# Normed rows transposed by halves of the tokens, and a first chunk that takes the first 256 tokens first

## The chip, the cores and the metric

One core of a Trainium2 chip runs the whole program in one launch. The metric is the device time of one execution in microseconds (us); the kernel before took 3114.05 us, the median of three runs (3106.38 to 3122.09).

## The reference

Two blocks of two layers on 512 tokens of 1024 features, in fp32. What matters here is what stands between the layers: the sum of a layer's input and output is normed row by row, and the next layer begins with a matrix product of these rows.

```python
def layer_norm(x, g, b):
    mu = mean(x, -1); var = mean(square(x - mu), -1)
    return (x - mu) * rsqrt(var + LN_EPS) * g + b

h = layer_norm(x, ln_in_g, ln_in_b)                      # passage 1
for l in range(2):                                       # first block
    hcat = h @ w_in[l] + b_in[l]                         # 7168 columns, attention and gating on them
    ...
    h = layer_norm(ALPHA * h + merged @ w_out[l] + b_out[l], ln_g[l], ln_b[l])   # passages 2 and 3
for l in range(2):                                       # second block
    p = h @ w_in_2[l]                                    # four recurrent mixers on its columns
    ...
    h = layer_norm(ALPHA * h + mix, ln1_g[l], ln1_b[l])  # passages 4 and 6
    f = swiglu(h) if l == 0 else moe(h)
    h = layer_norm(ALPHA * h + f, ln2_g[l], ln2_b[l])    # passage 5, and the output
```

So there are six passages from normed rows into a product with weights. The sixth goes into the router of the mixture of experts.

## The kernel before

Rows of the 512 tokens lie in four tiles of 128 tokens, `H[t][0]` and `H[t][1]`, each 128x512 (512 features). Products want the features on the partitions, so every normed tile is transposed on TensorE, eight blocks of 128x128 a tile, into PSUM banks (`norm_transpose`, L495). A bank holds 128x512, one block `k` of 128 features for all 512 tokens; seven banks are open at once, and the eighth block waits for one to come free. An fp32 product is made of three fp32r products: `split` (L412 to L415) casts a transposed block to a high part `hh` on ScalarE and subtracts it for a low part `hl` on VectorE; `weights` (L384) loads a chunk of 1024x256 as two transfers of 512 KB, casts each to `wh` on ScalarE (L395) and subtracts for `wl` on VectorE (L399); `mm3` (L406 to L408) multiplies `wh` by `hh`, `wh` by `hl` and `wl` by `hh`. (In the trace's names the operands stand as they come: L407 reads `hl`, L408 reads `wl`.) `proj_f` takes one half of a chunk, 128 output features, through all eight blocks: 24 matmuls of 512 columns into one of two PSUM banks of the tag `mm`.

The norm of a tile (`norm_rows`, `norm_apply`) runs over all engines: VectorE's statistics (L543, L1457 and their like) and aggregation (L454), the power on GpSimd (L439), then for the first half of the features two operations on VectorE (L467, L468) and for the second half one on ScalarE (L355), a product on GpSimd (L470) and a sum on VectorE (L485). `norm_end` then scales the rows (L515, ScalarE), adds a bias row at some passages (L518, GpSimd) and writes them to memory (L520, SyncE's queue), for the next residual.

Each engine runs its instructions in one order, written by a scheduler at build time that models when each could start. `BEHIND`, `FREE` and `HELD` (L33 to L35) steer it: the first `wl` of the first chunk is free, the next four are held behind the split number `BEHIND`. What follows the first chunk: at passages 1 and 2 `naqkv` (L592, VectorE), at 3 and 5 `shift` (L1513 on ScalarE, L1515 to L1517 on VectorE), at 4 a Silu on ScalarE (L355). These read the two `mm` banks and free them.

Of the kernel before, what the change touches and what calls it, by code (L numbers as in the profile page):

```python
# [19 lines left out]
P = 128  # L20
D = 1024
S = 512
KT = D // P
# [4 lines left out]
CW = 256  # L28
# [6 lines left out]
BEHIND = 3  # L35
# [5 lines left out]
PF, PS = (0, 1), (0,)  # L41
# [218 lines left out]
def _consts3():  # L260
# [16 lines left out]
T_R, T_K, T_V, T_WA, T_G, T_HF, T_HQ, T_LQ, T_LK, T_LR, T_HG, T_RQ, T_RK, T_RG = (  # L277
    0, 2, 4, 6, 7, 8, 10, 12, 13, 14, 16, 18, 20, 22)
# [36 lines left out]
class K:  # L315
# [104 lines left out]
    def proj_f(self, w, c0, hT, kt=KT):  # L420
# [4 lines left out]
            self.mm3(o, w[k][0][:, c0:c0 + P], w[k][1][:, c0:c0 + P], hh[:, k, :], hl[:, k, :], k == 0, k == kt - 1)  # L425
        return o

    def proj_t(self, w, width, t, hT, kt=KT, tag="mm"):

        o = self.bank(tag)  # L430
        hh, hl = hT
        for k in range(kt):
            self.mm3(o[:, :width], hh[:, k, t * P:(t + 1) * P], hl[:, k, t * P:(t + 1) * P],
                     *w[k], k == 0, k == kt - 1)
        return o[:, :width]
# [3 lines left out]
        self.nc.gpsimd.tensor_tensor(out, out, self.mhalf, op=ALU.pow)  # L439
        return i.ins  # L440

    def norm_begin(self, ng, nb, bo=None, keep=None, spill=False, tags="tsatsamt", pool=()):

        banks = [{"t": "tp", "s": "sc", "a": "av", "m": "mm"}[c] for c in tags]
        self.ln = SimpleNamespace(g=self.row(ng), b=self.row(nb), bo=None if bo is None else self.row(bo),
                                  keep=keep, spill=spill, tags=banks, tp={}, pool=pool, late=None,
                                  mv=self.xp.tile([P, 4, 2], F32, name="mv", tag="mv", bufs=2),
                                  rs=self.xp.tile([P, 4], F32, name="rs", tag="rs", bufs=2),
                                  sh=self.xp.tile([P, 4], F32, name="sh", tag="sh", bufs=2))
# [37 lines left out]
            for j in range(2):  # L487
                nc.sync.dma_start(ln.keep[j][t * P:(t + 1) * P, :], H[t][j])

    def norm_transpose(self, t, ks=range(7)):  # L490
        ln = self.ln
        for k in ks:
            if k not in ln.tp:
                ln.tp[k] = self.bank(ln.tags[k])
            self.nc.tensor.transpose(ln.tp[k][:, t * P:(t + 1) * P], self.H[t][k // 4][:, (k % 4) * P:(k % 4 + 1) * P],  # L495
                                     self.ident)

    def norm_end(self):

        nc, ln, H = self.nc, self.ln, self.H  # L500
        hh = self.xp.tile([P, KT, S], F32R, name="hh", tag="hh")
        hl = self.xp.tile([P, KT, S], F32R, name="hl", tag="hl")
        for t in range(4):
            self.norm_transpose(t)
        for k in range(KT):
            if k >= 7:
                for t in range(4):
                    self.norm_transpose(t, [k])
            i = self.split(hh[:, k, :], hl[:, k, :], ln.tp[k])
            if k == BEHIND:  # L510
                self.behind = (i.ins, FREE, HELD)
        for t in range(4):
            for j in range(2):
                h = H[t][j]
                nc.scalar.mul(h, h, ALPHA)  # L515
                if ln.bo is not None:
                    with self.tc.issue_after(ln.last_mul):
                        nc.gpsimd.tensor_add(h, h, ln.bo[j])  # L518
                if ln.spill:
                    nc.sync.dma_start(self.hd[j][t * P:(t + 1) * P, :], h)  # L520
        return hh, hl
# [49 lines left out]
    def hybrid(self, l, hT):  # L571
        nc, aps = self.nc, self.aps
# [12 lines left out]
        nq, nk, nv = [], [], []  # L585
        for c in range(0, 12, 2):
            w = chunk(c)
            for j in range(2):
                o = self.proj_f(w, j * P, hT)
                t = self.c("naqkv")  # L590
                (nq if c < 4 else nk if c < 8 else nv).append(t)
                nc.vector.tensor_scalar(t.rearrange("p (c r) -> p r c", r=8), o.rearrange("p (r c) -> p r c", c=64),  # L592
                                        bcol(c + j), -0.125 if c < 4 else 1.0, op0=ALU.add, op1=ALU.mult)
# [237 lines left out]
        nb = R_L + 5 * l  # L831
        self.norm_begin(nb, nb + 1, nb + 5 + 2 if l + 1 < DEPTH else None, spill=True)
        st = self.stats()
        for js in ((0,), (1,), (2, 3)):
            w = [self.weights(aps[f"wo1_{l}"][j], KT, CW) for j in js]
# [37 lines left out]
    def second_block(self, hT):  # L873
        nc, aps = self.nc, self.aps
        cst = self.cp.tile([P, 1154], F32, name="cst2")
        nc.sync.dma_start(cst, aps["cst2"][:, :1154])
        self.perm, self.blk1, self.cen = cst[:, 0:128], cst[:, 128:256], cst[:, 256:384]
        self.masks = cst[:, 384:512], cst[:, 512:640]
        self.reset = cst[:, 640:1152]
        self.sign = cst[:, 1152:1153]  # L880
        msk = self.cp.tile([P, 8 * P], mybir.dt.uint8, name="msk")
        for c0 in range(0, 8 * P, S):
            nc.gpsimd.tensor_copy(msk[:, c0:c0 + S], self.load(aps["msk2"][:, c0:c0 + S]))
        self.lvt = lambda n: msk[:, (1 + n) * P:(2 + n) * P]

        m64 = self.cp.tile([P, 12, 64], mybir.dt.uint8, name="m64")
        self.strict64 = self.cp.tile([P, 64], F32, name="strict64")
        nc.sync.dma_start(self.strict64, aps["cst3"][:, :64])
        nc.gpsimd.tensor_copy(m64[:, 6:12].rearrange("p n c -> p (n c)"), self.load(aps["cst3"][:, 64:448])[:, :384])
        self.ident64 = self.cp.tile([P, 64], F32, name="ident64")  # L890
        for h in (slice(0, 64), slice(64, P)):
            nc.gpsimd.tensor_copy(m64[h, :6], msk[h, P:7 * P].rearrange("p (n c) -> p n c", c=P)[:, :, h])
            nc.gpsimd.tensor_copy(self.ident64[h], self.ident[h, h])
        self.lvt64 = lambda n: m64[:, n]
        self.lv64 = lambda n: m64[:, 6 + n]
        self.fcol = {}
        for name, val in (("m_rms", RMS_EPS), ("m_ln", LN_EPS), ("m_lnx", 64e-5), ("one", 1.0),
                          ("b15", 15 * float(np.log(2.0)))):
            t = self.cp.tile([P, 1], F32, name=name)
            nc.vector.memset(t, val)  # L900
            self.fcol[name] = t
        self.ones = self.cp.tile([P, P], F32, name="ones")
        nc.vector.memset(self.ones, 1.0)
        h4 = self.cp.tile([P, 4], F32, name="h4")
        nc.vector.memset(h4, 0.0)
        for h in range(4):
            nc.vector.memset(h4[32 * h:32 * h + 32, h:h + 1], 1.0)
        self.heads = {2: self.blk1.rearrange("p (h c) -> p c h", c=64)[:, 0], 4: h4}
        self.rotary_tables()
        self.lower_bound()  # L910
        for l in range(DEPTH):
            v0 = V2_L + l * V2_LN
            self.v2 = lambda n, i=0, w=1: self.vec[:, v0 + V2[n] + i:v0 + V2[n] + i + w]
            self.hv2 = lambda n, i=0, w=1: self.hvec[:, v0 + V2[n] + i:v0 + V2[n] + i + w]
            nb = R2_L + 4 * l
            if l == 1:
                self.moe_begin()
            hT = self.mixers(l, hT)
            if l == 0:
                for i in range(2):  # L920
                    hT_ = self.swiglu(hT, aps[f"fgu_{i}"], aps[f"fd_{i}"], (nb + 2, nb + 3) if i else None)
                hT = hT_
            else:
                self.moe(hT, (nb + 2, nb + 3))
# [391 lines left out]
                put(main * P, P, j, y)  # L1316
                put(rest_col * P + own, R, j, t[:R])

    def swiglu(self, hT, wgu, wd, norm):

        nc = self.nc
        ah, al = [], []
        for m in range(11):
            w = self.weights(wgu[m], KT, CW)
            g = self.proj_f(w, 0, hT)
            s = self.tmp()
            self.act(s, g, AF.Silu)
            u = self.proj_f(w, P, hT)
            nc.vector.tensor_mul(s, s, u)
            ah.append(self.c("ah", F32R))  # L1330
            al.append(self.c("al", F32R))
            self.split(ah[m], al[m], s)
        if norm:
            self.norm_begin(*norm, spill=True, tags="smsmaatt", pool=PS)
            st = self.xp.tile([P, 4, 2, 6], F32, name="st2", tag="st2", bufs=2)
        acc = {}
        order = [[(j, k0, kn)] for j in range(2) for k0, kn in ((0, 3), (3, 4))] + [[(0, 7, 4), (1, 7, 4)]]
        for part in order:
            w = [self.weights(wd[j][:, k0 * 512:(k0 + kn) * 512], kn, 512) for j, k0, kn in part]
            for t in range(4):  # L1340
                for (j, k0, kn), wj in zip(part, w):
                    if k0 == 0:
                        acc[j, t] = self.bank((("mm", "mm", "sc", "sc"), ("av", "av", "tp", "tp"))[j][t])
                    for k in range(kn):
                        ts = slice(t * P, t * P + P)
# [13 lines left out]
    def mixers(self, l, hT):  # L1359

        nc, aps = self.nc, self.aps
# [4 lines left out]
        hold = {}  # L1366
        self.y = {}

        def feat(t):
            if t % 2 == 0:  # L1370
                hold["w"] = self.weights(wf[t // 2], KT, CW)
            return self.proj_f(hold["w"], (t % 2) * P, hT)

        def tok(i, out):
            w = self.weights(aps[f"w2t_{l}"][i], KT, CW)
# [9 lines left out]
        k = [self.shift(feat(T_K + i), mu(2 + i)) for i in range(2)]  # L1385
# [9 lines left out]
        z = self.rwkv_common(v, wa, g1, g2)  # L1395
# [627 lines left out]
```

## Time and profile before

| | |
|---|---|
| median of 3 runs | 3114.05 us |
| the profiled execution's own time | 3123.69 us |
| its span | 3121.9 us |
| TensorE clock granted, mean | 0.968 |
| TensorE busy | 2969.5 us (95%) |
| VectorE busy | 1881.3 us (60%) |
| ScalarE busy | 1314.5 us (42%) |
| GpSimd busy | 357.0 us (11%) |

The six passages lie in the trace at 14 to 42, 605 to 629, 1198 to 1220, 1630 to 1654, 2006 to 2030 and 2437 to 2454 us: from about the last product of the old layer to the end of the first chunk of the new one. Times within the trace are from the start of the span. A row's duration reaches some 0.08 us into the next row of a busy engine, so that the pitch of a run of instructions is read from their starts.

### The profile page before, as it was taken

What the parts mean: (1) busy time and instruction counts of PE and PEld (TensorE: products, weight loads), DVE (VectorE), ACT (ScalarE), POOL (GpSimd) and SP (SyncE); (2) the same over time, 40 slices, a digit from 0 to 9 for tenths busy, and PEclk for the clock granted to TensorE, in tenths of its full rate; (3) what the DMA queues carried; (4) which work ended last, traced back from release to release, by engine and by line L of the source; (5) the groups of instructions that cost most, each with busy time, mean ns of one, the idle gap of its engine ahead of it and who ended that gap; (6) DMA issues with size and microseconds to landing.
All of it is one profiled execution on the core that took longest, in us unless ns stands there. A gap on an engine that the chain in (4) does not pass through costs nothing. (4 is left out here: it accounts for less than half of the span.)

```text
span 3121.9 us, 46921 instructions
## 1 busy us (share of the span) xinstructions
PE 2969.5 (95%) x18729; PEld 2426.4 (78%) x18729; DVE 1881.3 (60%) x3318; ACT 1314.5 (42%) x2257; POOL 357.0 (11%) x377
## 2 busy tenths in 40 slices
PE   7999999999999999998999999999999799999987
PEld 5688788877878888786668888778775699999973
DVE  6676554657745566636574333555467777777765
ACT  3534332335433333524433222343354466666642
POOL 3220000211100001004210000100232200000021
PEclk9999999999999999999899999999999899999997
DMA  5322224242221333210303233321121378777772
GB/s 187 103 81 81 71 65 148 79 148 78 75 80 49 122 122 115 75 41 16 102 28 101 88 102 95 130 90 43 35 68 62 130 250 265 255 250 258 250 260 87
DMA packets 116535, 365.69 MB, mean 117 GB/s; under 512 B 13585, under 2 KB 16785, under 8 KB 116305
## 3 DMA queue, kind: packets, MB, share of 16 engines
q1 hardware_dynamic: 113424, 353.13, 35.0%
q0 software_dynamic: 2880, 9.44, 0.9%
q8 instruction: 150, 2.46, 0.3%
q14 instruction: 81, 0.66, 0.1%
HBM read 344.83 MB, written 17.69 MB: 116 GB/s over the span
## 5 line engine op out<-in xcount | busy, mean ns | idle before, releaser
L399 DVE TENSOR_TENSOR wl<-wr,wh 128x1024 fp32r<-128x1024 f32 (+1 forms) x574 | 696.9, 1223 | 519.6 <-ACT wh L395 514.0
L395 ACT CAST wh<-wr 128x1024 fp32r<-128x1024 f32 (+1 forms) x574 | 594.2, 1045 | 754.0 <-PE mm L407 340.3
L406 PE MATMUL mm<-hh,wh 128*128 128x512 f32 (+1 forms) x1616 | 652.2, 404 | 0.1
L407 PE MATMUL mm<-hl,wh 128*128 128x512 f32 (+1 forms) x1616 | 645.2, 399 | 0.0
L408 PE MATMUL mm<-hh,wl 128*128 128x512 f32 (+1 forms) x1616 | 642.0, 398 | 0.1
L406 PEld LDWEIGHTS mm<-hh,wh 128*128 128x128 f32 (+1 forms) x1616 | 306.3, 190 | 75.0 <-issue 7.1
L408 PEld LDWEIGHTS mm<-hh,wl 128*128 128x128 f32 (+1 forms) x1616 | 305.7, 189 | 73.3 <-issue 4.3
L407 PEld LDWEIGHTS mm<-hl,wh 128*128 128x128 f32 (+1 forms) x1616 | 306.1, 189 | 69.9 <-issue 5.6
L1266 PE MATMUL mm<-xgT,wh 128*128 128x320 f32 x704 | 219.1, 311 | 2.1 <-issue 2.1
L1266 PE MATMUL sc<-xgT,wh 128*128 128x320 f32 x704 | 218.7, 311 | 1.1 <-issue 1.1
L1267 PE MATMUL mm<-xgT,wl 128*128 128x256 f32 x704 | 197.6, 281 | 4.1 <-issue 4.1
L1267 PE MATMUL sc<-xgT,wl 128*128 128x256 f32 x704 | 197.6, 281 | 2.7 <-issue 2.7
L1266 PEld LDWEIGHTS mm<-xgT,wh 128*128 128x128 f32 x704 | 133.1, 189 | 4.3 <-issue 3.6
L1266 PEld LDWEIGHTS sc<-xgT,wh 128*128 128x128 f32 x704 | 133.1, 189 | 4.2 <-issue 4.2
L1267 PEld LDWEIGHTS mm<-xgT,wl 128*128 128x128 f32 x704 | 133.3, 189 | 2.3 <-issue 2.0
L1267 PEld LDWEIGHTS sc<-xgT,wl 128*128 128x128 f32 x704 | 133.0, 189 | 2.3 <-issue 2.3
L406 PE MATMUL mm<-wh,hh 128*128 128x256 f32 x448 | 130.8, 292 | 0.6 <-DVE sgv L754 0.6
L439 POOL TENSOR_TENSOR rs<-rs,mhalf 128x1 f32<-128x1 f32 x36 | 29.7, 824 | 889.3 <-DVE rs L438 858.8
L407 PE MATMUL mm<-wl,hh 128*128 128x256 f32 x448 | 129.2, 288 | 0.0
L408 PE MATMUL mm<-wh,hl 128*128 128x256 f32 x448 | 128.4, 287 | 0.0
L728 DVE TENSOR_REDUCE mn<-sc 128x1 f32<-128x512 f32 x64 | 44.1, 689 | 86.0 <-PE sc L725 85.7
L355 ACT ACTIVATE tmp<-mm,hvec 128x512 f32<-128x512 f32 x72 | 49.4, 686 | 96.1 <-PE mm L408 96.1
(554 smaller groups left out, 5674.8 us busy)
## 6 DMA issues: line engine op xcount, KB each, us to landing
wr<-mgu SPq DMA_DIRECT2D x176, 512.0 KB
wr<-w SPq DMA_DIRECT2D x172, 512.0 KB
wr<-md SPq DMA_DIRECT2D x88, 512.0 KB
wr<-fgu SPq DMA_DIRECT2D x44, 512.0 KB
wr<-wo SPq DMA_DIRECT2D x32, 512.0 KB
wr<-wbr SPq DMA_DIRECT2D x24, 512.0 KB
row<-rows SPq DMA_DIRECT2D x40, 256.0 KB
wr<-fd SPq DMA_DIRECT2D x20, 512.0 KB
```

Source lines behind the costliest of these rows:

```text
L355: i = self.nc.scalar.activation(out, src, f, **kw)
L395: nc.scalar.copy(hi[:, :n], raw[:, :n])
L399: nc.vector.tensor_sub(lo[:, :n], raw[:, :n], hi[:, :n].bitcast(F32))
L406: mm(out, lh, rh, start=first, stop=False)
L407: mm(out, lh, rl, start=False, stop=False)
L408: mm(out, ll, rh, start=False, stop=last)
L439: self.nc.gpsimd.tensor_tensor(out, out, self.mhalf, op=ALU.pow)
L728: nc.vector.tensor_reduce(mx[u][:, a:a + 1], sc, axis=AX.X, op=ALU.min)
L1266: mm(o[i][:, :2 * CAP], wh, x[:, k, :2 * CAP], start=k == 0, stop=False)
L1267: mm(o[i][:, :256], wl, x[:, k, :256], start=False, stop=k == KT - 1)
```

## The change

A bank now holds two blocks of 128 features for 256 tokens: bank (half, kp) takes blocks 2kp and 2kp+1 of the tokens of tiles 0 and 1, or 2 and 3. `norm_end` transposes tiles 0 and 1, splits their four banks, then transposes tiles 2 and 3 and splits theirs: eight splits of 128x2x256 in place of eight of 128x512. `self.behind` is set to the last split of the first half. A new function, `proj_first`, takes both halves of a first chunk together, the first 256 tokens through all blocks, then the last 256: 96 matmuls of 256 columns in place of 48 of 512, in two `mm` banks that are both open to its end. It is called at passages 1 to 5; the router of passage 6 is as it was, but takes its rows through the new `norm_end`.

```diff
+    def proj_first(self, w, hT):
+        o = [self.bank("mm") for _ in range(2)]
+        hh, hl = hT
+        for n in range(2):
+            ts = slice(n * CW, (n + 1) * CW)
+            for k in range(KT):
+                for j in range(2):
+                    self.mm3(o[j][:, ts], *(x[:, j * P:(j + 1) * P] for x in w[k]), hh[:, k, ts], hl[:, k, ts],
+                             k == 0, k == KT - 1)
+        return o
...
-    def norm_begin(self, ng, nb, bo=None, keep=None, spill=False, tags="tsatsamt", pool=()):
+    def norm_begin(self, ng, nb, bo=None, keep=None, spill=False, tags="ttssaatt", pool=()):
...
-    def norm_transpose(self, t, ks=range(7)):
+    def norm_transpose(self, t):
         ln = self.ln
-        for k in ks:
-            if k not in ln.tp:
-                ln.tp[k] = self.bank(ln.tags[k])
-            self.nc.tensor.transpose(ln.tp[k][:, t * P:(t + 1) * P], self.H[t][k // 4][:, (k % 4) * P:(k % 4 + 1) * P],
+        for k in range(KT):
+            z = t // 2, k // 2
+            if z not in ln.tp:
+                ln.tp[z] = self.bank(ln.tags[4 * z[0] + z[1]])
+            c = 2 * (k % 2) + t % 2
+            self.nc.tensor.transpose(ln.tp[z][:, c * P:(c + 1) * P], self.H[t][k // 4][:, (k % 4) * P:(k % 4 + 1) * P],
                                      self.ident)
...
-        for t in range(4):
-            self.norm_transpose(t)
-        for k in range(KT):
-            if k >= 7:
-                for t in range(4):
-                    self.norm_transpose(t, [k])
-            i = self.split(hh[:, k, :], hl[:, k, :], ln.tp[k])
-            if k == BEHIND:
+        for half in range(2):
+            for t in (2 * half, 2 * half + 1):
+                self.norm_transpose(t)
+            for kp in range(4):
+                hi, lo = (x[:, 2 * kp:2 * kp + 2, half * CW:(half + 1) * CW] for x in (hh, hl))
+                i = self.split(hi, lo, ln.tp[half, kp].rearrange("p (k n) -> p k n", k=2))
+            if half == 0:
                 self.behind = (i.ins, FREE, HELD)
...
             w = chunk(c)
+            first = self.proj_first(w, hT) if c == 0 else None
             for j in range(2):
-                o = self.proj_f(w, j * P, hT)
+                o = first[j] if first else self.proj_f(w, j * P, hT)
...
-            g = self.proj_f(w, 0, hT)
+            if m == 0 and new:
+                g, u = self.proj_first(w, hT)
+            else:
+                g, u = self.proj_f(w, 0, hT), None
             s = self.tmp()
             self.act(s, g, AF.Silu)
-            u = self.proj_f(w, P, hT)
+            u = u or self.proj_f(w, P, hT)
...
-            return self.proj_f(hold["w"], (t % 2) * P, hT)
+                if t == T_R:
+                    hold["o"] = self.proj_first(hold["w"], hT)
+            return hold["o"][t - T_R] if t < T_R + 2 else self.proj_f(hold["w"], (t % 2) * P, hT)
```

What the scheduler makes of it is seen in the order of each engine. The line numbers after the change are higher: L467, L468 and L485 become L479, L480 and L497, L438 and L454 become L450 and L466, L458 becomes L470, L515 becomes L530. In the three places below `hh` and `hl` are the high and low parts of the rows, `wh` and `wl` those of the weights, `tp`, `sc`, `av` and `mm` are tags of PSUM banks, and `x4` says that four such instructions follow each other.

First, ScalarE at passage 1. Before, the cast of the first chunk's weights stands ahead of the eight casts of rows:

```order
L515 ACTIVATE H<-H 128x512
L395 CAST wh<-wr 128x1024
L515 ACTIVATE H<-H 128x512
L414 CAST hh<-tp 128x512
L414 CAST hh<-sc 128x512
L414 CAST hh<-av 128x512
```

Now, on the same engine, it stands behind all of them and behind the scalings of the rows:

```order
L530 ACTIVATE H<-H 128x512 x2
L414 CAST hh<-tp 128x2x256
L355 ACTIVATE H<-H,sh,rs 128x512
L414 CAST hh<-tp 128x2x256
L414 CAST hh<-sc 128x2x256 x2
L530 ACTIVATE H<-H 128x512
L414 CAST hh<-av 128x2x256 x2
L414 CAST hh<-tp 128x2x256 x2
L530 ACTIVATE H<-H 128x512 x5
L395 CAST wh<-wr 128x1024 x4
```

What moved is the first `wh`, from ahead of the first `hh` to behind the last scaling.

Second, VectorE at passage 1. Before, with the first `wl` ahead of the splits:

```order
L468 SCALAR_TENSOR_TENSOR H<-H,rs,row 128x512
L485 TENSOR_TENSOR H<-H,row 128x512
L399 TENSOR_TENSOR wl<-wr,wh 128x1024
L415 TENSOR_TENSOR hl<-tp,hh 128x512
L415 TENSOR_TENSOR hl<-sc,hh 128x512
L415 TENSOR_TENSOR hl<-av,hh 128x512
```

Now, VectorE from the last tile's sum (L497) to the weights of the first two chunks:

```order
L497 TENSOR_TENSOR H<-H,row 128x512
L415 TENSOR_TENSOR hl<-tp,hh 128x2x256
L415 TENSOR_TENSOR hl<-sc,hh 128x2x256 x2
L415 TENSOR_TENSOR hl<-av,hh 128x2x256 x2
L415 TENSOR_TENSOR hl<-tp,hh 128x2x256 x2
L597 TENSOR_SCALAR qg<-vec 128x1 x2
L984 TENSOR_TENSOR lbt<-vec 128x2
L1622 TENSOR_SCALAR oma<-vec 128x1 x2
L985 TENSOR_TENSOR lbt<-vec,lbt 128x2
L986 TENSOR_TENSOR lbt<-vec,lbt 128x2
L1008 TENSOR_TENSOR fold<-cst 16x8
L399 TENSOR_TENSOR wl<-wr,wh 128x1024 x4
```

Here the first `wl` moved behind the splits and behind a row of small operations on tables; one split stands ahead of L480 of the last tile, seven behind its sum. Six operations on tables and then the third chunk's `wl` follow, and only then the first `naqkv`.

Third, VectorE at passage 4, from the last tile's residual sum. Before:

```order
L1455 TENSOR_TENSOR H<-mm,H 128x512
L1457 BN_STATS st_13224<-H 128x6
L454 BN_AGGR mv<-st_13224 128x2
L438 TENSOR_SCALAR rs<-mv 128x1
L485 TENSOR_TENSOR H<-H,row 128x512
L458 SCALAR_TENSOR_TENSOR sh<-mv,rs 128x1
L467 SCALAR_TENSOR_TENSOR H<-H,mv,row 128x512
L468 SCALAR_TENSOR_TENSOR H<-H,rs,row 128x512
L485 TENSOR_TENSOR H<-H,row 128x512
L415 TENSOR_TENSOR hl<-tp,hh 128x512
```

Now, on the same engine and from the same sum:

```order
L1476 TENSOR_TENSOR H<-mm,H 128x512
L1478 BN_STATS st_13368<-H 128x6
L415 TENSOR_TENSOR hl<-tp,hh 128x2x256
L466 BN_AGGR mv<-st_13368 128x2
L415 TENSOR_TENSOR hl<-tp,hh 128x2x256
L450 TENSOR_SCALAR rs<-mv 128x1
L497 TENSOR_TENSOR H<-H,row 128x512
L470 SCALAR_TENSOR_TENSOR sh<-mv,rs 128x1
L479 SCALAR_TENSOR_TENSOR H<-H,mv,row 128x512
L415 TENSOR_TENSOR hl<-sc,hh 128x2x256
L480 SCALAR_TENSOR_TENSOR H<-H,rs,row 128x512
L497 TENSOR_TENSOR H<-H,row 128x512
```

Three splits of the first half moved between the steps of the last tile's norm; the other five come behind its last sum, and behind those the `wl` of the chunk's second half. Passages 5 and 6 have the same three splits there; passages 2 and 3 have one, between L479 and L480. On TensorE, at passages 4 and 5, 28 of the 96 matmuls of `proj_first` stand ahead of the first one that reads the second half of `wl`, and nearly as many ahead of the last tile's last four transposes; at 2 and 3 there are 11 ahead of these. At passages 3 and 5 VectorE runs L1536, L1537 and L1536 of both banks before the first L1538 that frees one.

## Rows read from the trace of the kernel before

**Rows 1.** The page, busy time by engine: us, share of the span, instructions

```profile
PE 2969.5 (95%) x18729; PEld 2426.4 (78%) x18729; DVE 1881.3 (60%) x3318; ACT 1314.5 (42%) x2257; POOL 357.0 (11%) x377
```

**Rows 2.** Waits of PE: line waited for, us in total, times, longest

```profile
PE sc L495 <- DVE H L485: 16.1, 11, 3.2
```

**Rows 3.** Timeline of PE, matmuls of 256 and 512 columns: start, us, instruction, idle before

```profile
605.48 0.28 PE L407 MATMUL mm<-wl,mh 128*128 128x256 f32 x1
605.60 0.28 PE L408 MATMUL mm<-wh,ml 128*128 128x256 f32 x1
...
625.45 0.39 PE L407 MATMUL mm<-hl,wh 128*128 128x512 f32 x1
625.68 0.39 PE L408 MATMUL mm<-hh,wl 128*128 128x512 f32 x1
```

**Rows 4.** Timeline of DVE (VectorE) at passage 1

```profile
23.52 1.75 DVE L485 TENSOR_TENSOR H<-H,row 128x512 f32<-128x512 f32 x1
25.19 2.29 DVE L399 TENSOR_TENSOR wl<-wr,wh 128x1024 fp32r<-128x1024 f32 x1
27.41 0.68 DVE L415 TENSOR_TENSOR hl<-tp,hh 128x512 fp32r<-128x512 f32 x1
...
32.19 0.85 DVE L968 TENSOR_TENSOR lbt<-vec 128x2 f32<-128x2 f32 x1
...
35.49 4.61 DVE L399 TENSOR_TENSOR wl<-wr,wh 128x1024 fp32r<-128x1024 f32 x4
```

**Rows 5.** Timeline of ACT (ScalarE) at passage 1

```profile
21.87 1.03 ACT L395 CAST wh<-wr 128x1024 fp32r<-128x1024 f32 x1
...
29.78 2.71 ACT L515 ACTIVATE H<-H 128x512 f32<-128x512 f32 x5
32.39 2.94 ACT L395 CAST wh<-wr 128x1024 fp32r<-128x1024 f32 x3
...
46.89 1.05 ACT L395 CAST wh<-wr 128x1024 fp32r<-128x1024 f32 x1 [9.28 <-DMA wr<-w]
```

**Rows 6.** Timeline of PE at passage 1

```profile
29.48 0.63 PE L408 MATMUL mm<-hh,wl 128*128 128x512 f32 x1
...
32.47 0.52 PE L406 MATMUL mm<-hh,wh 128*128 128x512 f32 x1
```

**Rows 7.** Timeline of SyncE's queue at passage 1

```profile
31.81 9.81 SPq L520 DMA_DIRECT2D hd<-H  x5
41.71 2.95 SPq L394 DMA_DIRECT2D wr<-w  x4
```

**Rows 8.** Timeline of DVE at passage 2, the second eviction of the first chunk

```profile
628.86 1.21 DVE L592 TENSOR_SCALAR naqkv<-mm,vec 128x512 f32<-128x512 f32 x1 [0.62 <-PE mm L408]
```

**Rows 9.** Timeline of DVE at passage 3, the first eviction

```profile
1217.09 0.69 DVE L1515 TENSOR_TENSOR sh<-tmp,mm 128x511 f32<-128x511 f32 x1 [2.03 <-ACT tmp L1513]
...
1217.88 0.75 DVE L1517 SCALAR_TENSOR_TENSOR sh<-sh,vec,mm 128x512 f32<-128x512 f32 x1
```

**Rows 10.** Timeline of DVE at passage 4

```profile
1637.37 0.75 DVE L468 SCALAR_TENSOR_TENSOR H<-H,rs,row 128x512 f32<-128x512 f32 x1
1639.28 0.69 DVE L485 TENSOR_TENSOR H<-H,row 128x512 f32<-128x512 f32 x1 [1.16 <-POOL H L470]
1639.89 0.68 DVE L415 TENSOR_TENSOR hl<-tp,hh 128x512 fp32r<-128x512 f32 x1
```

**Rows 11.** Timeline of POOL (GpSimd) at passage 4

```profile
1637.61 1.65 POOL L470 TENSOR_TENSOR H<-H,row 128x512 f32<-128x512 f32 x1 [1.12 <-ACT H L355]
```

**Rows 12.** Timeline of PE at passage 4

```profile
1641.87 0.78 PE L407 MATMUL mm<-hl,wh 128*128 128x512 f32 x1
...
1643.72 0.44 PE L408 MATMUL mm<-hh,wl 128*128 128x512 f32 x1
```

**Rows 13.** Timeline of DVE at passage 2, under a product on GpSimd

```profile
604.75 1.80 DVE L468 SCALAR_TENSOR_TENSOR H<-H,rs,row 128x512 f32<-128x512 f32 x1
```

**Rows 14.** Timeline of POOL at passage 2, at the same time

```profile
603.97 2.03 POOL L470 TENSOR_TENSOR H<-H,row 128x512 f32<-128x512 f32 x1 [1.12 <-ACT H L355]
```

More of the change, by code (lines that the diff above doesn't have):

```diff
@@ L920, in second_block @@
                 for i in range(2):
-                    hT_ = self.swiglu(hT, aps[f"fgu_{i}"], aps[f"fd_{i}"], (nb + 2, nb + 3) if i else None)
+                    hT_ = self.swiglu(hT, aps[f"fgu_{i}"], aps[f"fd_{i}"], (nb + 2, nb + 3) if i else None, i == 0)
                 hT = hT_
@@ L1317, in expert, with swiglu @@
                 put(rest_col * P + own, R, j, t[:R])
-    def swiglu(self, hT, wgu, wd, norm):
+    def swiglu(self, hT, wgu, wd, norm, new):
         nc = self.nc
@@ L1333, in swiglu @@
         if norm:
-            self.norm_begin(*norm, spill=True, tags="smsmaatt", pool=PS)
+            self.norm_begin(*norm, spill=True, tags="mmaasstt", pool=PS)
             st = self.xp.tile([P, 4, 2, 6], F32, name="st2", tag="st2", bufs=2)
```

## The prediction

> **What bounds the kernel now.** I read the page first: TensorE is busy 95% of the span, the other engines far less [rows 1]. A change is worth what it takes from or adds to TensorE's idle time. The waits come next: TensorE's largest wait at the norm passages is for L485 on VectorE, the sum that completes a tile, 16.1 us over 11 waits, the longest 3.2 [rows 2]. Then I read each passage engine by engine. The reader is to see there a chain: the last tile's sum on VectorE, its transposes, the splits, the weights' low part `wl`, and the first product. At passage 4 the last sum starts at 1639.28 and eight splits follow from 1639.89 [rows 10]; TensorE starts its first dense run at 1641.87, while VectorE is still splitting [rows 12]. So in the kernel before, the first product already overlaps the splits. What the change could take is the idle time before the last sum, and nothing in the product itself.
>
> **The cost of the matmuls.** 96 matmuls of 256 columns replace 48 of 512. One of 256 starts 0.12 us after the one before it (605.48 to 605.60), one of 512 0.23 us [rows 3]; over long runs 0.114 and 0.229. So the product costs the same, 11.0 us at full clock, and I put the doubled weight loads at nothing: in the stretch of 256 columns as many loads per column stand as `proj_first` has. The page "TensorE: Matmul & The Clock Gate" of the Trainium skill, in its section "Back-to-back issue gap", says that the spacing is set by load and matmul together, with a fixed part that weighs more on narrow matmuls; the trace shows no such part at 256 columns (0.12 against half of 0.23), so the sum by that rule would be the same within a microsecond a passage.
>
> Splits are as many as before and as large, eight of 128x512 elements. They write two runs of 256 rather than one of 512. I take the price of before, 0.60 us a piece on VectorE (27.41 to 32.19 is eight) [rows 4]. From below nothing makes them faster; from above, the nearest row with a split-up access is `naqkv`, 1.21 us against 0.68 [rows 8, 10]. That end is a rival below.
>
> **Passage 1, +7.0 us.** The first `wl` stood before the splits: it starts at 25.19 [rows 4], and TensorE's first L408, which reads it, at 29.48 [rows 6]. Now seven splits stand ahead of it after the last sum at 25.19: 25.2 + 7 x 0.60 = 29.4. Then the small operations, from 32.19 to 35.49, are 3.3 us [rows 4], to 32.8 with the two of `qg`; then `wl`, 1.15 (4.61 for four) [rows 4], about 34.0. Its other input is no later: the eight `hh` end by about 27.4, the five scalings take 2.6 (29.78 to 32.39), one cast of weights 1.0 [rows 5], so 31.0. L408 starts at 34.1, 4.6 late, and as the rest of the product costs the same, it ends at 46.0 in place of 41.4 (29.48, 46 matmuls at 0.229, and 1.4 us for the time to 32.47 at half clock, pitch 0.43 [rows 6]).
>
> Then both `mm` banks are full, and the first `naqkv` that frees one stands behind the third chunk's `wl`. That chunk's transfer is issued at 41.71, behind the row writes on SyncE's queue [rows 7], and its cast starts at 46.89 [rows 5], 5.2 us later. The scalings that start this chain run about 1.9 us earlier now, so I put the cast at 45.0, the cast and `wl` end at 47.2, and the eviction, 1.21 [rows 8], at 48.4: TensorE waits 2.4 us beyond 46.0. Together 7.0. Between: 6 if the transfer comes a microsecond earlier, 9 if the writes hold it as long as before. If the `wl` wait was hidden anyway, only the 2.4 is left.
>
> **Passage 2, +0.9 us (-0.5 to 2.5).** One split between L479 and L480 pushes the last tile by at most 0.6. TensorE has 11 of 96 matmuls done when the rest begins, which ends the product 0.3 earlier than before. Then it waits for one eviction, 1.21 [rows 8], which before lay beside the second half's matmuls.
>
> **Passage 3, +2.7 us (2 to 4.5).** The product ends at about the same time (+0.2). Then the first bank comes free only when ScalarE's copy, L1536 of both banks and the first L1538 are through: 0.6 for the copy, 0.60, 0.10, 0.60 and 0.70 on VectorE, pitches of the rows [rows 9]. That is 2.6, of which about 0.1 is covered. Before, the same work lay beside the second half's 5.5 us of matmuls.
>
> **Passage 4, +2.0 us (0.3 to 3).** Two splits now stand within the last tile's statistics: its sum comes 1.2 us later. A third stands ahead of L480. In the trace L468, its earlier name, starts at 1637.37 and GpSimd's product at 1637.61 [rows 10, 11], so the VectorE operation is through first; now it comes 0.6 behind the start of that product. What that costs is seen once in the trace: the same L468 takes 1.80 us rather than 0.75 [rows 10, 13] when it starts 0.78 into a product on GpSimd that ends at 606.00 [rows 14]. I take 0.5. The last sum then ends at 1639.9 + 1.7 = 1641.6, the five splits at 1644.6, `wl` of the second half at 1645.8. TensorE has 28 matmuls behind it by then, and has stood still: 68 are left, 68 x 0.116 = 7.9, to 1653.8 at full clock. Before, the product ended at 1653.7: 1641.87, 47 matmuls at 0.233, and 0.9 for the half clock until 1643.72 [rows 12]. If the clock has fallen in the wait, 1.9 is added; I take 1.5, and 0.5 for the Silu's read of the bank.
>
> The Trainium skill says the same of L480: in "SBUF — State Buffer", section "Who interferes with whom", VectorE with two operands in SBUF and GpSimd share a port that is locked for a whole instruction, the loser standing still. The trace agrees (1.80 against 0.75 above). By it the whole remaining product would be waited out, about 0.9 rather than 0.5 at passages 4 to 6, 1.2 us more in all.
>
> **Passage 5, +4.0 us (2.3 to 5).** The same delay as at 4, 1.5, and the same wait for two banks as at 3, 2.5.
>
> **Passage 6, +1.4 us (0.5 to 1.7).** The same two or three splits delay the last tile; the router has no `proj_first` that could use the early half.
>
> Where a lower end stands without a reason, it leaves out the estimated terms of that passage (the lock, the fallen clock); an upper end adds one more late operation of about 1.2 us, a `wl` [rows 4] or an eviction [rows 8].
>
> **Sum.** 7.0 + 0.9 + 2.7 + 2.0 + 4.0 + 1.4 = 18.0 us (bounds 10.6 to 25.7). On the profiled execution's 3123.69 us (span 3121.9 and 1.8 around it) that is 3141.7. This execution was 9.6 above the median, which has no part in the sum; on the median of 3114.05 it is 3132.
>
> **Rivals.** *The gain arrives (faster).* The first half's 48 matmuls, 5.5 us, run while the last tile is still being normed, at five places: 27 us less, 3087. For it: TensorE's waits for L485 (16.1 us [rows 2]) are filled, and a filled wait also keeps the clock up. Against: in VectorE's order only one split at passages 2 and 3 and three at 4 and 5 come before the last sum, so a quarter at most of the first half has its operands. I give 0.10, for 3080 to 3098.
>
> *Nothing gained, little lost (no change).* The early 28 matmuls at passages 4 and 5 keep the clock at full, so that the product ends 1 to 2 us earlier there, and the `wl` wait of passage 1 is shorter as VectorE's small operations are spread otherwise: 2.4 + 0.9 + 2.7 + 1 + 2.5 + 0.5 = 10, or as little as 5: about 3121. I give 0.25, for 3102 to 3122.
>
> *Splits are slower (more lost).* If the write or the read in two runs costs what `naqkv`'s access does, 0.53 us more a piece [rows 8, 10], five of them late at each of six passages are 16 us more: 3148. It would decide from the first split after the last sum. I give 0.10.
>
> My forecast has 0.55. Its own range is 3122 to 3146: the bounds of the sum, 3124.6 to 3139.8, and some microseconds on either side for the spread of medians.
>
> **How the numbers follow.** A difference of 0.5%, 15.6 us, is about what a measurement of this kernel can tell from no change: 3098.5 to 3129.6 is no change. Of my forecast's 0.55, 0.36 lies above 3129.6 and 0.19 below; the no-change rival adds its 0.25 to the same, the slow splits 0.10 to slower; the gain is faster: 0.10, 0.44 and 0.46. The range of 3107 to 3146 leaves out the gain and most of the slow splits.
>
> **What would show it.** In the new profile: `hl` of 128x2x256 at 0.60 apart; TensorE's first L408 at passage 1 at about 34; an idle of 2.5 us on TensorE behind the first chunk at passages 3 and 5, waiting for `sh` on VectorE; an idle of some 3 to 4 us in `proj_first` at passages 4 and 5, waiting for `wl`; the last tile's sum at passages 4 to 6 over a microsecond later after the last residual sum. I am wrong if the matmuls of the first half lie densely ahead of the last tile's transposes, or if the two banks are free when the second chunk's first matmul is due.

## The result, and the profile after

The changed kernel took 3129.80 us, the median of seven runs (3118.15 to 3136.51), against 3110.32 for the kernel before (seven runs, 3100.49 to 3122.09). The ratio is 1.0052, 95% interval 1.0032 to 1.0073: slower by 16 us (10 to 23); the two medians alone lie 19.5 apart. The forecast was 18 us slower.

The page of the profiled execution seems to say the opposite, since its span is shorter than before's 3121.9:

```profile
span 3116.3 us, 47414 instructions
PE 2955.7 (95%) x18969; PEld 2433.3 (78%) x18969; DVE 1883.1 (60%) x3318; ACT 1314.7 (42%) x2257; POOL 360.1 (12%) x377
```

That execution was the fastest of the seven. One stretch that the change doesn't touch, between passages 3 and 4, took it 9 us less than the execution of before. The windows show it, first of the kernel before, then of the changed one (us, busy time by engine, granted clock, share of the DMA engines, GB/s):

```profile
1507.00:1590.00 83.00, 76.28 (x267) 49.46 (x265) 56.81 (x139) 33.90 (x74) 19.52 (x26) 0.86 0.28 89
```

```profile
1514.00:1588.00 74.00, 67.19 (x270) 44.60 (x268) 57.08 (x139) 34.28 (x74) 20.03 (x26) 0.98 0.30 100
```

It is the same work in the same order: VectorE is busy for 57 us in both, TensorE for 76 and 67, at a granted clock of 0.86 and 0.98. In the seven profiles of the experiments below the same stretch was granted 0.98 twice, 0.93 once and 0.86 to 0.88 four times. So spans of single executions don't rank these kernels, and I compare the passages instead. The measure is the time from the start of the last tile's last statistics on VectorE to the second chunk's first matmul. At passage 3 the two ends are these rows, of the kernel before:

```profile
1200.68 0.43 DVE L529 BATCH_NORM_STATS2 st<-H 128x6 f32<-128x256 f32 x1
```

```profile
1219.94 0.39 PE L406 MATMUL mm<-hh,wh 128*128 128x512 f32 x1
```

They are 19.26 us apart. In the changed kernel the first is

```profile
1206.67 0.43 DVE L544 BATCH_NORM_STATS2 st<-H 128x6 f32<-128x256 f32 x1
```

and the second stands at 1228.64, so 21.97, and the difference is +2.71. "Product" is the same difference for the first chunk's end, "second chunk" for the second chunk's first matmul (at passage 6, with no chunk, the router's last matmul):

| passage | product | second chunk | forecast |
|---|---|---|---|
| 1 | +4.55 | +6.40 | +7.0 |
| 2 | -0.36 | +0.68 | +0.9 |
| 3 | +0.11 | +2.71 | +2.7 |
| 4 | -0.23 | +0.25 | +2.0 |
| 5 | +1.43 | +4.04 | +4.0 |
| 6 | -0.64 | -0.64 | +1.4 |
| sum | | +13.4 | +18.0 |

At passage 3 another 1.7 us come behind the second chunk's start, which makes 15.1.

Two differences lie outside these windows. Between passages 4 and 5 TensorE starts its matmuls of 512 columns 0.2333 us apart in the kernel before and 0.2289 in the changed one, at a granted clock of 1.00 in both; by passage 5 that is 2.0 us in favour of the changed kernel. Of the experiments below only halves alone has 0.2333 there too, but both spacings also turn up in other stretches from one execution to another, so that it is not shown whether the change does this. And behind passage 6 a `wl` of 1.21 us no longer stands between the router's first two operations on VectorE, which gives 0.8 us more. With both the sum is about 12.

**Passage 1.** Where the first `wl` began at 25.19 and the L408 that reads it at 29.48 [rows 4, 6], VectorE now has:

```profile
24.24 0.68 DVE L415 TENSOR_TENSOR hl<-tp,hh 128x512 fp32r<-128x512 f32 x1
...
27.24 1.27 DVE L415 TENSOR_TENSOR hl<-tp,hh 128x512 fp32r<-128x512 f32 x2
28.43 0.20 DVE L597 TENSOR_SCALAR qg<-vec 128x1 f32<-128x1 f32 x2
...
31.02 4.61 DVE L399 TENSOR_TENSOR wl<-wr,wh 128x1024 fp32r<-128x1024 f32 x4
...
44.94 1.23 DVE L399 TENSOR_TENSOR wl<-wr,wh 128x1024 fp32r<-128x1024 f32 x1 [6.42 <-ACT wh L395]
46.08 2.17 DVE L608 TENSOR_SCALAR naqkv<-mm,vec 128x512 f32<-128x512 f32 x2
```

ScalarE casts the weights for the `wl` at 44.94 when their transfer has landed:

```profile
43.86 1.05 ACT L395 CAST wh<-wr 128x1024 fp32r<-128x1024 f32 x1 [10.66 <-DMA wr<-w]
```

TensorE in that time:

```profile
31.11 0.41 PE L407 MATMUL mm<-hl,wh 128*128 128x256 f32 x1
32.28 0.80 PE L408 MATMUL mm<-hh,wl 128*128 128x256 f32 x2 [0.75 <-DVE wl L399]
...
45.38 0.28 PE L408 MATMUL mm<-hh,wl 128*128 128x256 f32 x1
47.36 0.47 PE L406 MATMUL mm<-hh,wh 128*128 128x512 f32 x1 [1.70 <-DVE naqkv L608]
```

The reader is to see both losses of the forecast: the splits and small operations ahead of `wl`, and at the end the eviction that stands behind a `wl` whose transfer was late. (The whole passage starts 0.95 us earlier in this execution: L485 at 23.52 [rows 4], L497 at 22.57.)

**Passage 3.** TensorE waits for the bank that the first L1538 frees (the profile names the L1537 before it, but TensorE goes on just behind the end of L1538 at 1228.50), then runs at the lower of its two clocks, 1.2 GHz (matmuls of 512 columns 0.43 us apart), until 1231.8:

```profile
1225.91 0.28 PE L408 MATMUL mm<-hh,wl 128*128 128x256 f32 x1
1228.64 0.77 PE L406 MATMUL mm<-hh,wh 128*128 128x512 f32 x1 [2.45 <-DVE sh L1537]
1229.21 0.63 PE L407 MATMUL mm<-hl,wh 128*128 128x512 f32 x1
...
1231.77 0.53 PE L407 MATMUL mm<-hl,wh 128*128 128x512 f32 x1
1232.13 0.39 PE L408 MATMUL mm<-hh,wl 128*128 128x512 f32 x1
```

VectorE in that time; before, L1517 of the first bank came 0.8 us behind its L1515 [rows 9], now another bank's L1536 stands between:

```profile
1226.50 0.69 DVE L1536 TENSOR_TENSOR sh<-tmp,mm 128x511 f32<-128x511 f32 x1 [0.86 <-ACT tmp L1534]
1227.10 0.15 DVE L1537 TENSOR_SCALAR sh<-tmp 128x1 f32<-128x1 f32 x1
1227.16 0.68 DVE L1536 TENSOR_TENSOR sh<-tmp,mm 128x511 f32<-128x511 f32 x1
1227.76 0.74 DVE L1538 SCALAR_TENSOR_TENSOR sh<-sh,vec,mm 128x512 f32<-128x512 f32 x1
```

**Passage 4.** VectorE, from the last tile's statistics to the second half's `wl`:

```profile
1632.24 0.69 DVE L1478 BATCH_NORM_STATS2 st<-H 128x6 f32<-128x512 f32 x1
1632.85 0.67 DVE L415 TENSOR_TENSOR hl<-tp,hh 128x512 fp32r<-128x512 f32 x1
1633.44 0.20 DVE L466 BATCH_NORM_AGGREGATE mv<-st 128x2 f32<-128x12 f32 x1
1633.56 0.64 DVE L415 TENSOR_TENSOR hl<-tp,hh 128x512 fp32r<-128x512 f32 x1
...
1636.64 1.58 DVE L480 SCALAR_TENSOR_TENSOR H<-H,rs,row 128x512 f32<-128x512 f32 x1
1638.14 0.68 DVE L497 TENSOR_TENSOR H<-H,row 128x512 f32<-128x512 f32 x1
...
1642.06 3.49 DVE L399 TENSOR_TENSOR wl<-wr,wh 128x1024 fp32r<-128x1024 f32 x3
```

TensorE had done its 28 early matmuls by then, and waited for that `wl`, 3.55 us:

```profile
1638.98 0.37 PE L407 MATMUL mm<-hl,wh 128*128 128x256 f32 x1
1639.18 0.60 PE L510 MATMUL tp<-cst,H 128*128 128x128 f32 x4
1643.33 0.50 PE L408 MATMUL mm<-hh,wl 128*128 128x256 f32 x2 [3.55 <-DVE wl L399]
1643.67 0.28 PE L406 MATMUL mm<-hh,wh 128*128 128x256 f32 x1
```

**Passage 5.** The same kind of wait, 3.23 us, but here TensorE comes out of it at 1.2 GHz (0.21 us a matmul of 256 columns):

```profile
2016.66 0.79 PE L408 MATMUL mm<-hh,wl 128*128 128x256 f32 x2 [3.23 <-DVE wl L399]
2017.25 0.41 PE L406 MATMUL mm<-hh,wh 128*128 128x256 f32 x1
2017.47 0.41 PE L407 MATMUL mm<-hl,wh 128*128 128x256 f32 x1
```

### The profile page after: what moved, and what is told of

Same layout as the page of the kernel before. It is cut to its first block, busy times and chain, and to the rows that moved or that the text cites. A ratio compares the mean times of both kernels' runs of the same rounds, so it can differ in the third digit from the quotient of the medians.

```text
span 3116.3 us, 47414 instructions
## 1 busy us (share of the span) xinstructions
PE 2955.7 (95%) x18969; PEld 2433.3 (78%) x18969; DVE 1883.1 (60%) x3318; ACT 1314.7 (42%) x2257; POOL 360.1 (12%) x377
## 5 line engine op out<-in xcount | busy, mean ns | idle before, releaser
L406 PE MATMUL mm<-hh,wh 128*128 128x512 f32 (+2 forms) x1696 | 665.5, 393 | 14.8 <-DVE sh L1537 4.9
L408 PE MATMUL mm<-hh,wl 128*128 128x512 f32 (+2 forms) x1696 | 655.6, 387 | 10.0 <-DVE wl L399 10.0
L407 PE MATMUL mm<-hl,wh 128*128 128x512 f32 (+2 forms) x1696 | 657.4, 388 | 0.9 <-DVE hl L415 0.9
L406 PEld LDWEIGHTS mm<-hh,wh 128*128 128x128 f32 (+1 forms) x1696 | 322.4, 190 | 87.1 <-issue 12.4
L408 PEld LDWEIGHTS mm<-hh,wl 128*128 128x128 f32 (+1 forms) x1696 | 321.9, 190 | 80.0 <-DVE wl L399 11.2
L407 PEld LDWEIGHTS mm<-hl,wh 128*128 128x128 f32 (+1 forms) x1696 | 322.6, 190 | 66.3 <-issue 5.3
L408 PE MATMUL mm<-wh,hl 128*128 128x256 f32 x448 | 127.5, 285 | 0.0
```

The source lines that it names most:

```text
L406: mm(out, lh, rh, start=first, stop=False)
L407: mm(out, lh, rl, start=False, stop=False)
L408: mm(out, ll, rh, start=False, stop=last)
```

## The experiments

The theory is that the loss has three parts: the late low part of the weights, both banks full behind the first chunk, and splits within the last tile's norm. What the early half of the tokens gains is lost again in the wait for the weights. Ratios are to the kernel before, with 95% intervals; passages are given as above, second chunk against the kernel before.

| kernel | median us | ratio | passages 1 to 6 | sum |
|---|---|---|---|---|
| changed | 3129.80 | 1.0052 (1.0032 to 1.0073) | +6.4 +0.7 +2.7 +0.3 +4.0 -0.6 | +13.4 |
| banks in turn | 3117.23 | 1.0023 (1.0004 to 1.0042) | +4.8 -0.2 +0.1 -0.2 +1.2 -0.6 | +5.2 |
| halves alone | 3111.06 | 1.0008 (0.9990 to 1.0026) | +4.6 +0.5 +0.3 +0.9 +0.5 -0.7 | +6.1 |
| weights between | 3111.44 | 1.0003 (0.9986 to 1.0020) | +0.3 -0.2 +1.6 -2.5 +0.3 -0.3 | -0.8 |
| banks and weights | 3099.97 | 0.9962 (0.9942 to 0.9983) | -0.8 -1.8 -0.6 -3.0 -2.3 -0.7 | -9.1 |
| the same again | 3106.90 | 0.9984 (0.9966 to 1.0002) | -0.6 -1.8 -1.2 -3.0 -2.3 -0.7 | -9.5 |
| late splits | 3130.48 | 1.0046 (1.0027 to 1.0064) | +7.2 +2.5 +4.0 +1.1 +3.3 -0.3 | +17.8 |
| late splits, banks and weights | 3114.34 | 0.9998 (0.9984 to 1.0013) | -0.6 +0.5 +1.0 +0.3 +0.8 -0.4 | +1.5 |

The first four experiments share one chip and its runs of the kernel before (median 3111.44), the last three another (3115.39). The changed kernel itself was measured beside its own runs of the kernel before, so experiments are compared with it by their ratios. Of every kernel the sum lies within the interval of its ratio, but these intervals reach 5 or 6 us to either side, and the passages are one execution each: they agree with the times and don't prove each other.

**Banks in turn.** In the last 256 tokens, one bank is finished before the other is begun.

```diff
-            for k in range(KT):
-                for j in range(2):
-                    self.mm3(...)
+            for k, j in [(k, j) for k in range(KT) for j in range(2)] if n == 0 else \
+                    [(k, j) for j in range(2) for k in range(KT)]:
+                self.mm3(...)
```

> Times here are of the second chunk's first matmul, from the last tile's last statistics on VectorE, as a difference from the kernel before; the changed kernel has +6.4, +0.7, +2.7, +0.3 and +4.0 us at passages 1 to 5. This kernel finishes the first bank before it begins the second in the last 256 tokens. Theory (both banks full at the end of the first chunk): the idle time behind the first chunk, 1.9, 1.1, 2.7, 0.5 and 2.7 us, falls to under 0.3 everywhere, so the differences become about +4.6, -0.4, +0.1, -0.2 and +1.4; with the half clock that follows the wait at passage 3 that is 9 to 10 us less than the changed kernel, about 3120. Rival (the second chunk waits for its own weights, and the bank only hides it): the differences stay within 0.5 of the changed kernel's, and the time at 3130.

The idle time behind the first chunk is gone at all five passages. TensorE at passage 3 goes from the last matmul of 256 columns into the second chunk at full clock:

```profile
1226.53 0.28 PE L408 MATMUL mm<-hh,wl 128*128 128x256 f32 x1
1226.65 0.39 PE L406 MATMUL mm<-hh,wh 128*128 128x512 f32 x1
1226.88 0.40 PE L407 MATMUL mm<-hl,wh 128*128 128x512 f32 x1
```

since VectorE is through with the first bank about half a microsecond before the second chunk wants it, and nothing of the second bank stands between:

```profile
1224.64 0.69 DVE L1536 TENSOR_TENSOR sh<-tmp,mm 128x511 f32<-128x511 f32 x1 [3.48 <-ACT tmp L1534]
1225.25 0.15 DVE L1537 TENSOR_SCALAR sh<-tmp 128x1 f32<-128x1 f32 x1
1225.43 0.75 DVE L1538 SCALAR_TENSOR_TENSOR sh<-sh,vec,mm 128x512 f32<-128x512 f32 x1
```

The differences are those expected, to 0.3 us, and the time came out 9 us less than the changed kernel's by the ratios, as expected. The product's end moved by no more than 0.3 us (+4.8, -0.2, +0.1, -0.2, +1.2), so the wait was for the bank, and the rival falls.

**Halves alone.** The new `norm_end`, and `proj_f` everywhere.

```diff
-            first = self.proj_first(w, hT) if c == 0 else None
+            first = None
...
-            if m == 0 and new:
+            if False:
...
-                if t == T_R:
-                    hold["o"] = self.proj_first(hold["w"], hT)
-            return hold["o"][t - T_R] if t < T_R + 2 else self.proj_f(hold["w"], (t % 2) * P, hT)
+            return self.proj_f(hold["w"], (t % 2) * P, hT)
```

> The split by halves of the tokens stays, the first chunk goes through all 512 tokens as before, one bank after the other. Theory (the loss has three parts: the late weights, the full banks, the splits in the last tile's norm): no idle time behind the first chunk, but TensorE begins 1 to 2 us later than before, since block 0 now needs the fifth split; the second chunk's first matmul is 4 to 5 us late at passage 1 and 0.5 to 2.5 at 2 to 5; total about 10 us over before, 3120. Rival (the early half is worth what the wait costs): 3130 or more. Rival (the joint first chunk is the whole loss): as before, 3110.

Passages 2 to 5 lose 0.3 to 0.9, near or under the low end of the expectation; TensorE begins 0.5 to 1.4 us later there. Passage 1 loses the same 4.6 as the changed kernel's product does, so that loss comes with the split by halves and the order it leads to, not with the joint chunk. The time, 1.0008, lies nearer to the rival's no change than to the expected 3120, whose 10 us are outside the interval (3 less to 8 more), as is the other rival's 3130. The interval holds both 0 and the 6 us of the passages: by the time alone it stays undecided whether the joint chunk is the whole loss, the passages speak against it.

**Weights between.** `norm_end` loads and splits the first chunk's weights behind the first half's splits.

```diff
-    def norm_end(self):
+    def norm_end(self, src=None):
...
             if half == 0:
                 self.behind = (i.ins, FREE, HELD)
+                self.first_w = None if src is None else self.weights(src, KT, CW)
...
-            w = chunk(c)
+            w = chunk(c) if c else self.first_w
...
```

> The first chunk's weights are loaded and split between the splits of the first and of the second half, at passages 1 to 5; all else as in the changed kernel. Theory: the wait of TensorE for the weights' low part goes, 3.6 us at passage 4, 3.2 at 5 (down to under 1, since the fifth split is then awaited), and the first chunk at passage 1 starts 3 to 5 us earlier; passages 2 and 3 stay within 0.5; in all 7 to 11 us less than the changed kernel, about 3121. Rival (the last tile's sum and the five late splits bound the product anyway): passages 4 and 5 gain under 1 us, and only passage 1 moves: 3126.

At passage 4 the wait for `wl` falls from 3.55 to 0.82 us:

```profile
1644.24 0.50 PE L408 MATMUL mm<-hh,wl 128*128 128x256 f32 x2 [0.82 <-DVE wl L399]
```

and at passage 1 TensorE's first L408 starts at 27.55 rather than 32.28:

```profile
27.55 0.80 PE L408 MATMUL mm<-hh,wl 128*128 128x256 f32 x2 [0.53 <-DVE wl L399]
```

Against the changed kernel the passages gain 6.1, 0.9, 1.1, 2.7 and 3.7: 14, more than the 7 to 11 expected, and the time moved by as much. Passage 1 gave more than the range, and passages 2 and 3, where I expected nothing, gained about 1 us each: in the changed kernel TensorE waits for `wl` there too, 1.65 and 0.84 us, and here it doesn't. The rival falls.

**Banks and weights.** Both edits.

> Both of the two edits before. Theory (the two losses are independent): the sum of both gains, 16 to 20 us less than the changed kernel, 3110 to 3114, that is as before within 0.2%; the second chunk starts +1, 0, 0, -2 and -1 us against before at passages 1 to 5. Rival (one uncovers the other): under 12 us less than the changed kernel.

> The kernel with banks in turn and weights between the halves once more, beside these two on one chip: 0.996 of the kernel before, 0.994 to 0.998.

The gains add up, 22.5 us of the passages (13.4 to -9.1) against 8.2 and 14.2 of the two edits alone, and more than the 16 to 20 expected. The kernel is faster than the one before in the first series, 0.9962. In the second, 0.9984, it is so only just: that misses the expected 0.994 to 0.998, and the interval reaches 1. VectorE and TensorE at passage 4 now follow each other closely; VectorE:

```profile
1636.34 0.68 DVE L497 TENSOR_TENSOR H<-H,row 128x512 f32<-128x512 f32 x1
1636.94 0.68 DVE L415 TENSOR_TENSOR hl<-sc,hh 128x512 fp32r<-128x512 f32 x1
1637.54 1.21 DVE L399 TENSOR_TENSOR wl<-wr,wh 128x1024 fp32r<-128x1024 f32 x1
1638.67 1.28 DVE L415 TENSOR_TENSOR hl<-av,hh 128x512 fp32r<-128x512 f32 x2
```

The `wl` stands between the two halves' splits, where TensorE needs it.

**Late splits**, on the changed kernel, and then with banks and weights.

```diff
-            nc.vector.tensor_add(H[t][1], H[t][1], ln.b[1])
+            ln.last_add = nc.vector.tensor_add(H[t][1], H[t][1], ln.b[1]).ins
...
-                i = self.split(hi, lo, ln.tp[half, kp].rearrange("p (k n) -> p k n", k=2))
+                with self.tc.issue_after(ln.last_add):
+                    i = self.split(hi, lo, ln.tp[half, kp].rearrange("p (k n) -> p k n", k=2))
```

> The changed kernel with all eight splits on VectorE put behind the last tile's last sum, so that nothing of the first half of the tokens is ready early. Theory (in the changed kernel the early half buys nothing, since TensorE then waits for the weights' low part): the first chunk ends within 1 us of where the changed kernel's does at passages 2 to 5 (at 4 some 0.5 us later, at 5 some 1 us earlier), and the time stays at 3127 to 3133. Rival (the early half earns its 28 matmuls, 3.3 us at each of passages 4 and 5, which other losses hide): the first chunk ends 3 us later at both, and the time is 3136.

> The same edit made to the kernel that finishes the banks in turn and has the first weights between the halves. Theory (the early half is worth something as soon as the weights and the banks don't wait): the first chunk ends 2 to 3 us later than in that kernel at passages 4 and 5, 1 to 2 later at 2 and 3, in all 6 to 10 us: about 3108. Rival (the gain of that kernel is from the weights and the banks alone): it stays within 2 us, at 3100.

On the changed kernel nothing is gained or lost that the time can tell, 1.0046 against 1.0052; the passages lose 4.4 us in all. The product ends 0.9 later at passage 4 and 0.7 earlier at 5, as expected; at 2 and 3 it ends 1.2 and 1.3 later, a little over the 1 us that was given. On the kernel with both edits the passages lose 11 us (-9.5 to +1.5), at passages 4 and 5 3.2 and 3.1, and in all a little more than the 6 to 10 expected. At passage 4 the two ends are, with the splits early (the same again):

```profile
1631.53 0.69 DVE L1479 BATCH_NORM_STATS2 st<-H 128x6 f32<-128x512 f32 x1
```

```profile
1648.01 0.40 PE L406 MATMUL mm<-hh,wh 128*128 128x512 f32 x1
```

and with the splits late:

```profile
1627.37 0.69 DVE L1480 BATCH_NORM_STATS2 st<-H 128x6 f32<-128x512 f32 x1
```

```profile
1647.06 0.40 PE L406 MATMUL mm<-hh,wh 128*128 128x512 f32 x1
```

So at passages 4 and 5 the early half is worth 3 us when neither the weights nor the banks wait, and little in the changed kernel, where both do. With only one of the two waits gone it was not tried. The times point the same way, 0.9998 against 0.9984 on one chip, but their intervals overlap.

The third part of the theory has no experiment of its own. Late splits brings the last tile's last sum at passages 4 and 5 back to 4.9 us behind its statistics, as in the kernel before, and yet the product doesn't end earlier at 4, since the early matmuls are gone too. What the splits within the norm cost by themselves is not shown.

## Why the prediction was right, point by point

The size, 18 against 16 (10 to 23), came out right, and so did three of the six terms within 0.3 us. The rest of the agreement is partly luck: passages 4 and 6 lost 3.8 us less than forecast, and the half clock at passage 3 (1.7), which was not forecast, takes part of this back. By the passages the loss is 12 to 15 us; the runs can't tell this from 18.

- *Matmuls of 256 columns cost the same.* Nearly: 0.118 us apart in `proj_first` against half of 0.229, so 0.3 us a passage, a tenth of the loss. "TensorE: Matmul & The Clock Gate" of the Trainium skill, section "Back-to-back issue gap", says that narrow matmuls cost more than their columns alone, which I put aside. But the width alone doesn't explain it here: at passage 1 of weights between the same matmuls start 0.113 apart.
- *Splits at 0.60.* Right: 28.43 - 24.24 is seven in 4.19 us. The rival of slower splits is out.
- *Passage 1, +7.0; measured +6.4.* The product's end was put 4.6 late and was 4.55, but by two errors that cancel: L408, put 4.6 late, is 3.75 late (32.28; the 29.48 of before is 28.53 by this execution's time), and then TensorE stays at half clock until 37.2, 5 us rather than 3. The wait for the bank was put at 2.4 and was 1.9. Weights between takes 6.1 of it back.
- *Passages 2 and 3, +0.9 and +2.7; measured +0.7 and +2.7.* Banks in turn removes the idle time at once. Not forecast: TensorE's waits for `wl` in these products, 1.65 and 0.84 us, which the early matmuls made up for, and the half clock that follows the wait at passage 3, 1.7 us more.
- *Passage 4, +2.0; measured +0.25.* Here the term was mis-sized twice. The last sum was put 1.7 late; from its statistics it is 5.90 in place of 4.92 (1639.28 [rows 10] from 1634.36), 0.98 late. L480 did run into GpSimd's product and took 1.58 in place of 0.75, more than the 0.5 that I took: "SBUF — State Buffer" of the Trainium skill, "Who interferes with whom", had this right. But the sum behind it waited 1.16 us for that same product before [rows 10], and the third split and the longer L480, 1.4 us together, mostly filled this wait. At passages 5 and 6 the sum is as late, 0.95, where I had looked for over a microsecond. Then I took 1.5 of a possible 1.9 for a clock that falls while TensorE waits; at passage 4 it did not fall.
- *Passage 5, +4.0; measured +4.0.* The same two terms; here the clock fell, which cost about 1.9, and the wait for the bank was 2.5. That the total fits is luck in part: the last sum was less late than put and the clock cost more.
- *Passage 6, +1.4; measured -0.6.* The router's first matmul is 0.55 late, but only four of its sixteen start at half clock, where ten did before. I had no term for that. The `wl` that no longer stands among the router's operations gives 0.8 more, so the change gains there where I forecast a loss.
- *The rival of the gain.* Its early matmuls came, 28 of them, and late splits, on the kernel with both edits, shows them to be worth 3 us at each of passages 4 and 5, once `wl` and the banks don't take it back. "A quarter at most of the first half" was too low: over half of its 48 ran early there.

## What to carry to other kernels

When a change makes one operand early, look in each engine's order for the next operand of the same instruction, here the weights' low part: the gain goes as far as that one. When two outputs are built up together, the first consumer of either comes at the end of both, so let the last part finish them in turn. And compare passages, from one unchanged instruction to another, when single executions differ by more than the effect.

## What the runs showed of the hardware

The clock in a wait was not the same from place to place. Before its wait of 3.55 us at passage 4 TensorE had come up to full clock at 1638.3, about a microsecond earlier, and was at full clock behind it. At passage 5 it had run at full clock since the first early matmul at 2006.8, waited 3.23 us and came out at half for 3.8 us; its later wait there, 2.45 us, 6 us after the clock had come back, cost no clock, and the same 2.45 us at passage 3, some 11 us after, cost 1.7. In other runs the same wait of 2.45 us was followed by half clock only about a microsecond after TensorE had gone on at full clock (weights between, passages 3 and 5), or by none at all (late splits, passages 3 and 5). So this cost changes from run to run, and I have not read a rule from it. In the stretch from 1507 to 1590 us the granted clock lay between 0.86 and 0.98 from one execution to another, 9 us from end to end; why is open. And at full clock matmuls of the same shape start at one of two spacings through a whole stretch: 0.2289 or 0.2333 us with 512 columns, 0.113 or 0.118 with 256. What decides is open too.
